# Seams around the up projection: first panels begun inside the output projection, x1 streamed by tile, tails in pieces

## The chip, the cores and the metric

One core of a Trainium2 chip runs one layer of a streaming encoder in one launch. The metric is the device time of one execution in microseconds (us). The median of three timed runs of the kernel before is 2146.97 us, from 2144.51 to 2148.34. Beside these runs one execution was profiled; its trace is what the rows below come from.

## The reference

There are 1152 rows of 1024 values (1024 of a new stream, 8 x 16 of running streams), in float32. The mixers (gated linear attention and differential attention) make `mixed`; what the change touches comes behind them:

```python
x = layer_norm(ALPHA * x + mixed @ w_out, ln1_g, ln1_b)      # w_out 1024 x 1024
up = x @ w_up                                                # w_up 1024 x 5632
a, gate = split(up, [2816])
a_full = concatenate([left, a])                              # left: the last 2 rows of before
a_conv = conv_b
for j in range(3):
    a_conv = a_conv + a_full[:, j:j + t] * conv_w[j]
h = gelu(a_conv) * gate
x = layer_norm(ALPHA * x + h @ w_down, ln2_g, ln2_b)         # w_down 2816 x 1024
ffn_new = a_full[:, -2:]
```

## The kernel before

Every float32 product is made of three matmuls of halves: `split` (lines 91 to 96) makes a rounded high part on ACT (L93, DVE at L95) and the rest on DVE (L96), and `mm3` (lines 86 to 89) issues high x high (L87), one with a low moving part (L88 or L89) and one with a low weight part. So every operand that TensorE reads has first gone through a cast and a subtraction.

The order of the instructions on each engine is fixed when the program is built: a scheduler in the tile framework takes the program as written and sets, engine by engine, what stands behind what. At run time each engine goes through its own list and waits where a semaphore tells it to. A tile pool with n buffers lets the writer of use n+1 wait for the readers of the first. TensorE does matmuls and transposes; ACT casts, copies out of PSUM and does the gelu; DVE subtracts, adds and convolves; POOL does additions and small copies; SP issues all DMAs in one queue.

Output projection (lines 745 to 836). Nine row tiles t of 128 rows. `o_prep(t)` loads `mr`, transposes it (L763) and splits it into `mth` and `mtl`. The eight k slices of w_out come through two `wor` buffers (L797) and are split into `woh` and `wol`. For each tile two PSUM tiles `opp` of 512 columns take 24 matmuls each. DVE adds the residual (L812), `layer_norm` follows (L736, L737), `x1_d` receives the tile (L817), and the tile is transposed (L822). Up to row 576 the transpose is split into the operands of products 1 and 2, and is also copied to `r11` and `r12`; from there on it goes to `r21` and `r22` (L830). POOL forms sums and differences of these (L833 to L836), in place.

Up projection (lines 839 to 914). Rows and inner dimension are halved, and the a and gate columns of one panel take the place of the halves of a matrix product with seven products instead of eight. For each of 22 panels f, `ra` and `rg` bring 128 columns of a and 128 of gate (512 KB each, L852 and L854, two buffers `raw`). POOL forms four weight sums (L858 to L861), which with three unchanged blocks are the weights of products 1, 2, 6, 5, 7, 4 and 3; they are split into `wv` (10 buffers). A product is 24 matmuls of 288 columns, in two PSUM tiles (c = 0 and 1): products 1, 6, 7 and 4 accumulate in `ux`, 5 and 3 in `uy`, product 2 in another `uy`. ACT copies the running sum out where it is wanted (L883 to `ab`, L888 and L893 to `gt`, L897 and L899 to `ab`) and DVE adds the other (L886, L894, L901). The a part lies in `ab` (one buffer, with the two rows to its left, L870 and L871); POOL copies its last rows to `tails` (L903, L904); DVE convolves it (L907, L908, two times L910 and L911); the gelu (L912), the gate (L913) and the store to `h_d` (L914) follow. The operands of products 6, 5, 7, 4 and 3 (`xh`, `xl`) are made in front of the loop by ten casts and ten subtractions over the tiles `r11` to `rs1`.

Down projection (lines 920 to 1012). The 22 slices of h and of w_down come in groups of 2, 4, 4, 4, 4 and 4; each group adds to `yacc`, which for the first group starts as x1, loaded at once (4.6 MB, L964), with L972 adding the first matmuls. After each of the first three groups `tails_out` transposes up to eight slices of `tails` (L953) through one PSUM buffer and writes the new convolution rows.

## Time and profile before

| what | us |
|---|---|
| median of three runs | 2146.97 |
| profiled execution | 2142.43 |
| its span | 2140.4 |
| TensorE busy (matmuls) | 2062.1 (96%) |
| DVE busy | 1107.4 (52%) |
| ACT busy | 787.6 (37%) |
| POOL busy | 454.5 (21%) |

The span is the time from the first to the last instruction that the profiler saw; the execution is 2.0 us longer, and the median of the runs is 4.5 us above the profiled one. Busy shares are averages over stages: the first 1200 us are the input projection and the mixers, the output projection goes from 1201 to 1317, the up projection from 1336 to 1834, the down projection from 1837 to 2131. Where TensorE is busy all the time, nothing that the other engines do is seen in the end; where it waits, the wait list tells for whom. Matmul rows start a step apart and overlap, so their spacing, not their duration, is what one costs.

### The profile page before, as it was taken

The page shows a single profiled execution, that of the slowest core. Times are in us where ns is not written, and L with a number is a line of the kernel's source. Part 1 is how long each engine was busy: PE and PEld are TensorE (multiplying, and loading weights), DVE is VectorE, ACT ScalarE, POOL GpSimd, SP SyncE. Part 2 cuts the span into 40 slices and gives each one's busy share as a digit, 9 for nine tenths or more (in the row PEclk, how much of TensorE's full clock was granted, in tenths as well). Part 3 has the DMA queues.
Part 4 walks back from the last instruction along what each step waited for, and adds up shares of the span by engine and source line. Part 5 has one row for each costly group of instructions (what it writes and reads, how often), then busy time and mean ns, then how long its engine had stood idle before and what let it go on. Part 6 is the DMA issues. An engine that isn't in the chain of part 4 may idle for free.

```text
span 2140.4 us, 34421 instructions
## 1 busy us (share of the span) xinstructions
PE 2062.1 (96%) x14088; PEld 1938.4 (91%) x14088; DVE 1107.4 (52%) x1848; ACT 787.6 (37%) x1750; POOL 454.5 (21%) x531
## 2 busy tenths in 40 slices
PE   7999999999999999999999996999999999699998
PEld 7999999999999999999989885999999999588886
DVE  4344444546536363655544376665555655544447
ACT  3233333244434354434545333333333333301122
POOL 0124233110111102201132206332323222000006
PEclk9999999999999999999999998899999999899999
DMA  5214304422132223322351731222222221712222
GB/s 168 56 23 116 99 25 124 124 53 72 53 106 63 82 49 83 92 72 64 40 123 25 238 128 59 71 72 83 72 74 71 72 83 62 266 56 85 85 84 89
DMA packets 186767, 185.30 MB, mean 87 GB/s; under 512 B 9136, under 2 KB 169228, under 8 KB 186594
## 3 DMA queue, kind: packets, MB, share of 16 engines
q1 hardware_dynamic: 186610, 183.11, 29.8%
q8 instruction: 111, 1.82, 0.4%
q14 instruction: 46, 0.38, 0.1%
HBM read 131.10 MB, written 51.98 MB: 86 GB/s over the span
## 4 chain that ended last, share of the span: by engine, by line
PE 85%; DMA 7%; DVE 5%; ACT 1%; issue 1%; POOL 0%; SPq 0%; DVEq 0%; ACTq 0%; POOLq 0%
PE mm L87 11%; PE mm L89 11%; PE mm L88 11%; PE ux L89 4%; PE ux L87 4%; PE ux L88 4%; PE dn L87 4%; PE dn L88 4%; PE dn L89 4%; PE uy L89 3%; PE uy L87 3%; PE uy L88 3%; PE po L657 3%; PE sc L625 2%; DMA out_prompt_diff_k<-krow 2%; PE sc L626 1%
## 5 line engine op out<-in xcount | busy, mean ns | idle before, releaser
L89 PE MATMUL mm<-whi,xl 128*128 128x256 f32 x1368 | 392.5, 287 | 0.0
L88 PE MATMUL mm<-wlo,xh 128*128 128x256 f32 x1368 | 392.1, 287 | 0.0
L87 PE MATMUL mm<-whi,xh 128*128 128x256 f32 x1368 | 391.3, 287 | 0.0
L89 PEld LDWEIGHTS mm<-whi,xl 128*128 128x128 f32 x1368 | 261.3, 191 | 2.6 <-issue 1.2
L88 PEld LDWEIGHTS mm<-wlo,xh 128*128 128x128 f32 x1368 | 261.3, 191 | 2.3 <-issue 1.0
L87 PEld LDWEIGHTS mm<-whi,xh 128*128 128x128 f32 x1368 | 260.8, 191 | 2.2 <-issue 0.6
L87 PE MATMUL ux<-xh,wv 128*128 128x288 f32 x704 | 208.2, 296 | 11.9 <-ACT wv L93 11.9
L89 PE MATMUL ux<-xh,wv 128*128 128x288 f32 x704 | 208.5, 297 | 3.7 <-DVE wv L96 3.7
L88 PE MATMUL ux<-xl,wv 128*128 128x288 f32 x704 | 208.3, 296 | 0.0
L89 PE MATMUL mm<-xh,wlo 128*128 128x384 f32 x576 | 196.2, 342 | 0.0
L87 PE MATMUL mm<-xh,whi 128*128 128x384 f32 x576 | 195.7, 340 | 0.2 <-DVE sg L699 0.2
L88 PE MATMUL mm<-xl,whi 128*128 128x384 f32 x576 | 195.8, 340 | 0.0
L87 PE MATMUL dn<-wdh,hh 128*128 128x512 f32 x396 | 152.6, 392 | 13.4 <-DVE yacc L972 12.1
L87 PE MATMUL uy<-xh,wv 128*128 128x288 f32 x528 | 156.0, 296 | 0.3 <-ACT wv L93 0.3
L88 PE MATMUL dn<-wdl,hh 128*128 128x512 f32 x396 | 154.9, 391 | 0.6 <-DVE wdl L96 0.6
L88 PE MATMUL uy<-xl,wv 128*128 128x288 f32 x528 | 155.4, 295 | 0.0
L89 PE MATMUL dn<-wdh,hl 128*128 128x512 f32 x396 | 154.2, 391 | 1.1 <-DVE hl L96 1.1
L89 PE MATMUL uy<-xh,wv 128*128 128x288 f32 x528 | 155.1, 295 | 0.0
L87 PEld LDWEIGHTS ux<-xh,wv 128*128 128x128 f32 x704 | 133.1, 189 | 12.4 <-ACT wv L93 12.3
L89 PEld LDWEIGHTS ux<-xh,wv 128*128 128x128 f32 x704 | 133.0, 189 | 4.0 <-DVE wv L96 4.0
L88 PEld LDWEIGHTS ux<-xl,wv 128*128 128x128 f32 x704 | 133.2, 189 | 0.0
L632 ACT ACTIVATE e<-sc,mx 128x256 f32<-128x256 f32 (+7 forms) x128 | 94.2, 741 | 90.8 <-DVE mx L628 76.2
(322 smaller groups left out, 4478.7 us busy)
## 6 DMA issues: line engine op xcount, KB each, us to landing
fraw<-in_w_up SPq DMA_DIRECT2D x44, 512.0 KB, 4.1
raw<-in_w_in SPq DMA_DIRECT2D x38, 512.0 KB, 6.3
raw<-in_w_in SPq DMA_DIRECT2D x52, 256.0 KB, 5.6
h_d<-cv SPq DMA_DIRECT2D x22, 576.0 KB, 2.9
hr<-h_d SPq DMA_DIRECT2D x22, 576.0 KB, 5.0
fraw<-in_w_down SPq DMA_DIRECT2D x22, 512.0 KB, 4.9
og_d<-orow SPq DMA_DIRECT2D x4, 1152.0 KB, 10.0
od_d<-od SPq DMA_DIRECT2D x8, 576.0 KB, 3.5
```

Source lines behind the costliest of these rows:

```text
L87: nc.tensor.matmul(ps, lhsT=lh, rhs=rh, start=start, stop=False, skip_group_check=more)
L88: nc.tensor.matmul(ps, lhsT=lh, rhs=rl, start=False, stop=False, skip_group_check=more)
L89: nc.tensor.matmul(ps, lhsT=ll, rhs=rh, start=False, stop=stop, skip_group_check=more)
L625: nc.tensor.matmul(sc[:, c0:c0 + c], lhsT=Q[m][:, iq], rhs=KH[m][:, c0:c0 + c], start=True, stop=False)
L626: nc.tensor.matmul(sc[:, c0:c0 + c], lhsT=Q[m][:, iq], rhs=KLz[m][:, c0:c0 + c], start=False, stop=True)
L632: act(e[:, :nk], scs[m][:, :nk], AF.Exp, bias=mx[:, m:m + 1], accum_out=Z[:, i, m:m + 1])
L657: nc.tensor.matmul(po[:, 0, :], lhsT=wT[:, kt, :], rhs=v[:, kt, vc0:vc0 + P], start=kt == 0, stop=kt == i)
```

## The change

- `wpool` gets three `raw` buffers instead of two; `wor` loads through `raw` and the pool `ow` goes; `r` has three buffers instead of four.
- The PSUM pools change: `opp` (4) and `otp` (4) are shared by the output and the up projection, and the pool `mmp` of the stages before is closed ahead of them. The transposes of `o_prep` for t > 0 go to `otp` instead of `mm`.
- A class `Panel` holds a panel's work in pieces: loads and split of the first two weights (three buffers `w0` in a pool `ue` that is open during the output projection), the weight sums, the products. Panel 0 is loaded behind t = 6, its sums and the load of panel 1 behind t = 7, panel 0's products 1 and 2 stand in front of the last tile's transposes, panel 1's product 1 behind its sums. `wv` for the other five has 7 buffers.
- The operands of product 6 lie in a pool of their own, `r11` too, and are made first.
- x1 is loaded by row tile into two buffers, and the first group writes `yacc` from it; `hh`, `hl`, `wdh` and `wdl` become parts of one tile `hw`; the tails are written in pieces of four slices inside groups 1 to 3, through two PSUM buffers.

In the diff the methods of `Panel` that only repeat the loop body of before are left out.

```diff
-WV = 10
+WV = 7
...
-    wpool = ctx.enter_context(tc.tile_pool(name="wpool", bufs=2, reuse_waits="tile"))
+    wpool = ctx.enter_context(tc.tile_pool(name="wpool", bufs=3, reuse_waits="tile"))
...
+    class Panel:
+        def __init__(self, f):
+            self.f = f
+            ra = wpool.tile([P, D], F32, tag="raw", name="fraw")
+            nc.sync.dma_start(ra.rearrange("p (k n) -> p k n", k=KD), w_up[:, f * P:(f + 1) * P].rearrange("(k p) n -> p k n", p=P))
+            self.W = {}
+            for i, src in ((1, ra[:, :512]), (2, ra[:, 512:])):
+                self.weight(ue, "w0", 3, i, src)
+            self.ra = ra
+
+        def weight(self, pool, tag, bufs, i, src):
+            self.W[i] = pool.tile([P, 2, 512], F32R, tag=tag, name="wv", bufs=bufs)
+            split(self.W[i][:, 0, :], self.W[i][:, 1, :], src)
+
+        def first(self):
+            self.X = [opp.tile([P, 512], F32, tag="opp", name="ux") for _ in range(2)]
+            for _ in self.prod(1, self.X, True):
+                pass
+
+        def first_out(self):
+            f = self.f
+            self.ab = ab = ue.tile([P, SEQ + 2 + NS * 18], F32, tag="ab", name="ab")
+            self.abs_ = ab[:, SEQ + 2:].rearrange("p (s c) -> p s c", c=18)
+            G.memset(ab[:, 0:2], 0.0)
+            G.tensor_copy(self.abs_[:, :, 0:2], ccT[:, f])
+            for c in range(2):
+                nc.scalar.copy(ab[:, 2 + c * HN:2 + (c + 1) * HN], self.X[c][:, :HN])
+            for c in range(2):
+                V.tensor_tensor(ab[:, 2 + c * HN:2 + (c + 1) * HN], ab[:, 2 + c * HN:2 + (c + 1) * HN], self.Y[c][:, :HN], ALU.add)
...
-            raw = ow.tile([P, D], F32, tag="wor", name="wor")
+            raw = wpool.tile([P, D], F32, tag="raw", name="wor")
...
+            if t == 6:
+                panels[0] = Panel(0)
+            if t == 7:
+                panels[0].sums()
+                panels[1] = Panel(1)
+            if t == NT - 1:
+                panels[0].first()
+                panels[0].second()
+                panels[0].first_out()
             nc.sync.dma_start(x1_d[t * P:(t + 1) * P, :], r)
...
+            if t == NT - 1:
+                panels[1].first()
...
-    for i, r in ((6, "r11"), (5, "rs1"), (7, "r21"), (4, "r22"), (3, "r12")):
+    for pool, which in (("xvb", ((6, "r11"),)), ("xvc", ((5, "rs1"), (7, "r21"), (4, "r22"), (3, "r12")))):
...
     for f in range(NF):
+        if f > 1:
+            panels[f] = Panel(f)
+        p = panels.pop(f)
+        if f > 0:
+            p.sums()
+        p.weights()
+        if f > 1:
+            p.first()
+        if f > 0:
+            p.second()
+            p.first_out()
+        p.rest()
...
-            nc.sync.dma_start(yacc, x1_d.rearrange("(t p) c -> p t c", p=P))
...
+            if gi == 0:
+                x1, xn = xn, x1_load(t + 1) if t + 1 < NT else None
...
-                    V.scalar_tensor_tensor(yacc[:, t, cs], yacc[:, t, cs], ALPHA, ps, ALU.mult, ALU.add)
+                    V.scalar_tensor_tensor(yacc[:, t, cs], x1[:, cs], ALPHA, ps, ALU.mult, ALU.add)
...
-        if gi < 3:
-            tails_out(8 * gi, min(8, NF - 8 * gi))
+            if 0 < gi < 4 and t in (2, 6):
+                tails_out(4 * (2 * (gi - 1) + (t == 6)))
```

How the instructions stand is seen at three places. The first is SP's queue at the start of the output projection (`mix_d` is the last store of the mixers, `mr` the input of a row tile). Before, it reads:

```order
L797 DMA wor<-in_w_out 128x1024 x2
L705 DMA mix_d<-gm 128x256
L752 DMA mr<-mix_d 128x1024
L797 DMA wor<-in_w_out 128x1024 x2
L752 DMA mr<-mix_d 128x1024
L797 DMA wor<-in_w_out 128x1024 x2
```

The loads of two row tiles stand between the w_out loads there. In the changed kernel SP's queue reads at the same place:

```order
L901 DMA wor<-in_w_out 128x1024 x3
L705 DMA mix_d<-gm 128x256
L901 DMA wor<-in_w_out 128x1024 x2
L849 DMA mr<-mix_d 128x1024 x4
L930 DMA x_d<-r 128x1024
```

The loads of w_out go out three and two at a time, and those of the row tiles 1 to 4 now stand behind all of them.

The second is ACT at the seam between the output and the up projection, from the last tile's copies on. Before, with `r_12626` as r22, `rs_12627` as rs1, `r_12625` as r21, `r_12623` as r11 and `r_12624` as r12, it reads:

```order
L830 COPY r_12625<-otp 128x4x128
L830 COPY r_12626<-otp 128x4x128
L93 CAST xh_13572<-r_12626 128x1152 x2
L93 CAST xh_13560<-rs_12627 128x1152 x2
L93 CAST xh_13566<-r_12625 128x1152 x2
L93 CAST xh_13554<-r_12623 128x1152 x2
L93 CAST xh_13578<-r_12624 128x1152 x2
L93 CAST wv<-fraw 128x512 x2
L93 CAST wv<-ta 128x512 x2
```

The first weights stand behind the ten casts there. In the changed kernel ACT's list reads, with `r_12635` as r11, `rs_12634` as rs1, `r_12632` and `r_12633` as r21 and r22 and `r_12631` as r12:

```order
L93 CAST wv<-fraw 128x512 x2
L943 COPY r_12632<-otp 128x4x128
L943 COPY r_12633<-otp 128x4x128
L93 CAST xh_13667<-r_12635 128x1152 x2
L93 CAST xh_13677<-rs_12634 128x1152 x2
L93 CAST xh_13683<-r_12632 128x1152 x2
L93 CAST xh_13689<-r_12633 128x1152 x2
L93 CAST xh_13695<-r_12631 128x1152 x2
L93 CAST wv<-ta 128x512 x2
```

The weights of products 1 and 2 (`wv<-fraw`) have moved ahead of the last tile, and r11, which was fourth, is cast first.

The third is POOL in a panel of the up projection, the same eight rows over and over. Before, it reads:

```order
L870 MEMSET ab 128x2
L871 COPY ab<-ccT 128x8x2
L858 TENSOR_TENSOR ta<-fraw 128x512
L860 TENSOR_TENSOR tb<-fraw 128x512
L859 TENSOR_TENSOR ta<-fraw,ta 128x512
L861 TENSOR_TENSOR tb<-fraw,ta 128x512
L903 COPY tails<-ab 128x2
L904 COPY tails<-ab 128x16
```

The four sums (`ta`, `tb`) stand between the clearing of `ab` and the copies to `tails` there. In the changed kernel POOL's list reads:

```order
L795 MEMSET ab 128x2
L796 COPY ab<-ccT 128x8x2
L762 TENSOR_TENSOR ta<-fraw 128x512
L764 TENSOR_TENSOR tb<-fraw 128x512
L821 COPY tails<-ab 128x2
L822 COPY tails<-ab 128x16
L763 TENSOR_TENSOR ta<-fraw,ta 128x512
L765 TENSOR_TENSOR tb<-fraw,ta 128x512
```

Two of the sums have moved behind the `tails` copies, in front of the next clearing of `ab`.

## Rows read from the trace of the kernel before

**Rows 1.** The waits of TensorE: engine, line, awaited: us in total, times, longest.
```profile
PE dn L87 <- DVE yacc L972: 12.1, 1, 12.1
PE ux L87 <- ACT wv L93: 11.9, 1, 11.9
...
PE ft L953 <- DVE tr L954: 5.8, 2, 4.9
...
PE otp L822 <- DVE r L737: 5.3, 1, 5.3
...
PE dn L87 <- ACT hh L93: 1.3, 1, 1.3
```

**Rows 2.** Busy time by stretch (us, PE, PEld, DVE, ACT, POOL, clock, DMA).
```profile
1190.00:1230.00 40.00, 37.83 (x208) 30.52 (x207) 16.58 (x20) 16.19 (x23) 6.64 (x6) 1.00 0.68 212
1317.00:1344.00 27.00, 5.88 (x22) 4.56 (x21) 22.65 (x18) 15.09 (x20) 15.69 (x10) 0.58 0.05 19
1344.00:1800.00 456.00, 456.00 (x3427) 456.00 (x3426) 264.08 (x409) 165.90 (x349) 144.62 (x164) 0.99 0.24 75
```

**Rows 3.** Timeline of a full panel: start, us, engine, line, operation, [idle before].
```profile
1547.86 0.29 PE L87 MATMUL uy<-xh,wv 128*128 128x288 f32 x1
...
1548.44 0.81 DVE L907 TENSOR_SCALAR cv<-ab,cw,cb 128x1024 f32<-128x1024 f32 x1 [3.17 <-ACT ab L897]
...
1550.03 1.28 DVE L910 SCALAR_TENSOR_TENSOR cv<-ab,cw,cv 128x1024 f32<-128x1024 f32 x1
...
1554.02 0.34 DVE L911 SCALAR_TENSOR_TENSOR cv<-ab,cw,cv 128x128 f32<-128x128 f32 x1
...
1555.25 1.17 ACT L912 ACTIVATE cv<-cv 128x1152 f32<-128x1152 f32 x1
1556.32 0.69 ACT L883 COPY ab<-ux 128x288 f32<-128x288 f32 x2
...
1557.66 0.29 PE L87 MATMUL ux<-xh,wv 128*128 128x288 f32 x1
...
1563.42 1.29 POOL L858 TENSOR_TENSOR ta<-fraw 128x512 f32<-128x512 f32 x1 [8.39 <-DMA fraw<-in_w_up]
...
1566.62 1.14 DVE L96 TENSOR_TENSOR wv<-fraw,wv 128x512 fp32r<-128x512 f32 x1
1570.70 0.81 DVE L907 TENSOR_SCALAR cv<-ab,cw,cb 128x1024 f32<-128x1024 f32 x1 [2.94 <-ACT ab L897]
```

**Rows 4.** Timeline of an early panel, DVE and then POOL.
```profile
1389.30 1.10 DVE L907 TENSOR_SCALAR cv<-ab,cw,cb 128x1024 f32<-128x1024 f32 x1 [3.38 <-ACT ab L897]
1390.33 1.32 DVE L908 TENSOR_SCALAR cv<-ab,cw,cb 128x128 f32<-128x128 f32 x1
...
1392.17 2.31 DVE L910 SCALAR_TENSOR_TENSOR cv<-ab,cw,cv 128x1024 f32<-128x1024 f32 x1
...
1397.19 0.34 DVE L911 SCALAR_TENSOR_TENSOR cv<-ab,cw,cv 128x128 f32<-128x128 f32 x1
...
1389.81 1.75 POOL L859 TENSOR_TENSOR ta<-fraw,ta 128x512 f32<-128x512 f32 x1
1391.64 1.76 POOL L861 TENSOR_TENSOR tb<-fraw,ta 128x512 f32<-128x512 f32 x1
```

**Rows 5.** The chain that ended last, start of the output projection: start, us.
```profile
1202.61 6.39 DMA wor<-in_w_out
...
1226.61 0.92 PE opp L87 x4
```

**Rows 6.** Timeline of the seam: ACT, POOL, TensorE.
```profile
1325.12 2.20 ACT L93 CAST xh<-r 128x1152 fp32r<-128x1152 f32 x2
...
1328.88 2.26 POOL L835 TENSOR_TENSOR r<-rs,r 128x512 f32<-128x512 f32 x1
...
1342.97 0.61 PE L89 MATMUL ux<-xh,wv 128*128 128x288 f32 x1 [3.70 <-DVE wv L96]
```

**Rows 7.** DMA issues of the page: count, KB each, us to landing.
```profile
fraw<-in_w_up SPq DMA_DIRECT2D x44, 512.0 KB, 4.1
```

More of the change, by code (lines that the diff above doesn't have):

```diff
@@ L739 @@
     xr_s = ctx.enter_context(ExitStack())
     xv_s = ctx.enter_context(ExitStack())
+    up_s = ctx.enter_context(ExitStack())
     XH, XL = {}, {}
+    panels = {}
     with ExitStack() as os_:
-        opp = os_.enter_context(tc.tile_pool(name="opp", bufs=4, space=PSUM, reuse_waits="tile"))
-        otp = os_.enter_context(tc.tile_pool(name="otp", bufs=2, space=PSUM, reuse_waits="tile"))
+        otp0_s = os_.enter_context(ExitStack())
+        otp0 = otp0_s.enter_context(tc.tile_pool(name="otp0", bufs=2, space=PSUM, reuse_waits="tile"))
@@ L756, in o_prep @@
                 if t == 0:
+                    tp = otp0.tile([P, 512], F32, tag="otp", name="otp")
+                else:
                     tp = otp.tile([P, 512], F32, tag="otp", name="otp")
-                else:
-                    tp = mmp.tile([P, 512], F32, tag="mm", name="mm")
                 tp = tp.rearrange("p (i c) -> p i c", i=4)
@@ L767, in r_load @@
         def r_load(t):
[L768 removed]
+            r = op.tile([P, D], F32, tag="r", name="r", bufs=3)
             nc.sync.dma_start(r, x_rows(t))
@@ L791 @@
         variant(xv, 2)
-        R = {n: xr.tile([P, KD // 2, HT], F32, tag=n, name=n) for n in ("r11", "r12", "r21", "r22", "rs1")}
+        R = {n: xr.tile([P, KD // 2, HT], F32, tag=n, name=n) for n in ("r12", "r21", "r22", "rs1")}
+        R["r11"] = xr1.tile([P, KD // 2, HT], F32, tag="r11", name="r11")
         woh = oc.tile([P, KD, D], F32R, name="woh")
@@ L836 @@
                 G.tensor_tensor(R["r12"][:, :, c], R["r12"][:, :, c], R["r11"][:, :, c], ALU.subtract)
-    ms.close()
+            if t == NT - 1:
+                panels[1].first()
     us_ = ctx.enter_context(ExitStack())
-    xb = xv_s.enter_context(tc.tile_pool(name="xvb", bufs=1, reuse_waits="tile"))
-    for i, r in ((6, "r11"), (5, "rs1"), (7, "r21"), (4, "r22"), (3, "r12")):
-        variant(xb, i)
-        for k in range(0, KD // 2, 2):
-            split(XH[i][:, k:k + 2, :], XL[i][:, k:k + 2, :], R[r][:, k:k + 2, :])
+    for pool, which in (("xvb", ((6, "r11"),)), ("xvc", ((5, "rs1"), (7, "r21"), (4, "r22"), (3, "r12")))):
+        xb = xv_s.enter_context(tc.tile_pool(name=pool, bufs=1, reuse_waits="tile"))
+        for i, r in which:
+            variant(xb, i)
+            for k in range(0, KD // 2, 2):
+                split(XH[i][:, k:k + 2, :], XL[i][:, k:k + 2, :], R[r][:, k:k + 2, :])
+        xr1_s.close()
@@ L921, with x1_load @@
     dn = ctx.enter_context(tc.tile_pool(name="dnp", bufs=6, space=PSUM, reuse_waits="tile"))
-    ft = ctx.enter_context(tc.tile_pool(name="ftp", bufs=1, space=PSUM, reuse_waits="tile"))
+    ft = ctx.enter_context(tc.tile_pool(name="ftp", bufs=2, space=PSUM, reuse_waits="tile"))
+    def x1_load(t):
+        x1 = fp.tile([P, D], F32, tag="x1", name="x1", bufs=2)
+        nc.sync.dma_start(x1, x1_d[t * P:(t + 1) * P, :])
+        return x1
     def down_load(f):
@@ L945, with tails_out @@
     yacc = fc.tile([P, NT, D], F32, name="yacc")
[L947 to L954 removed]
+    def tails_out(f0):
+        fn = min(4, NF - f0)
+        tr = fc.tile([18, 512], F32, tag="tr", name="tr", bufs=2)
+        tp = ft.tile([P, 4, P], F32, tag="ft", name="ft")
+        for j in range(fn):
+            nc.tensor.transpose(tp[:18, j, :], tails[:, f0 + j, :], ident)
+        V.tensor_copy(tr[:, :fn * P], tp[:18, :fn, :].rearrange("p f c -> p (f c)"))
         cols = slice(f0 * P, (f0 + fn) * P)
```

144 lines of the change are left out of this document (68 added, 76 removed).

## Prediction, made before the changed kernel was run

> **What bounds the kernel now.** I read TensorE's waits first, then the busy times by stretch, then the timeline of the three places that the change touches. The list of waits [rows 1] shows where TensorE stands still, and it names two groups that the change aims at. At the seam between output projection and up projection it waits 5.3 us for the last layer norm and 11.9 for the first weight cast; the stretch from 1317 to 1344 holds only 5.88 us of matmuls at a mean granted clock of 0.58 [rows 2], so part of it ran at the lower of the two levels (1.2 and 2.4 GHz). At the down projection it waits 12.1 us for the first accumulation, which waits for the 4.6 MB load of x1, and 5.8 for the tail transposes. In between, the up projection leaves nothing to win: from 1344 to 1800 TensorE is busy 456.00 of 456.00 us [rows 2]. A change can only lose there.
>
> And the cover in that full stretch is short. Product 6 of a panel accumulates into the PSUM tiles of product 1, so it waits until ACT has copied these into `ab`; the copy waits until the convolution of the panel before is done with the one `ab` buffer. One such turn [rows 3]: product 4 ends and product 3 starts at 1547.86; DVE's convolution runs from 1548.44 to the end of its last step at 1554.36, 5.92 us with two weight splits in it; then come the gelu and, at 1556.32, ACT's two copies; product 6 starts at 1557.66. These 9.80 us are 74 matmuls of 0.1325 us each (9.80 / 74). Of them 0.58 pass before the convolution starts, and 1.55 behind it at best (the gelu's 1.17, the first copy's 0.35, and 0.03 between): the convolution may last 9.80 - 0.58 - 1.55 = 7.67 us before TensorE stops. In this panel POOL makes its four weight sums from 1563.42 on, after the convolution and product 6's start.
>
> An early panel shows what these sums cost when they meet the convolution [rows 4]. Two of the four lie beside it, 1.75 and 1.76 us long instead of 1.29; DVE's 128-column step takes 1.32 us, more than the 1024-column step ahead of it; the `ab`-by-`cv` step takes 2.31 instead of 1.28; the chain lasts from 1389.30 to 1397.53, 8.23 us. Two sums cost it 8.23 - 5.92 = 2.31, some 1.15 each. No stall came of it there, as that panel still had 12 more matmuls (the next panel's product 1) ahead of its product 6.
>
> **A. Start of the output projection: +4.** Before, tiles 0 and 1 share each k of w_out as it arrives; a load into one of the two buffers took 6.39 us at 1202.61 [rows 5], and still 37.83 of the 40 us from 1190 to 1230 are busy [rows 2]. After, tile 1 stands behind all but four of tile 0's 48 matmuls, which are 48 x 0.23 = 10.9 us of work (0.92 / 4, the step of a 512-column matmul [rows 5]). With three buffers the five late loads need about two trips of 6.4 us and a cast and split of some 2 behind each (an estimate from the casts' 1.1 in [rows 6]), 17 us in all; the 24 gate matmuls that now stand behind the first transposes cover 24 x 0.115 = 2.8 (half the columns, half the step). That leaves 17 - 10.9 - 2.8 = 3, and the loads for tiles 1 to 4 stand behind those of w_out on SP: I take +4, bounds 0 (the third buffer pays for it) and +8 (the gate's matmuls cover nothing).
>
> **B. Seam to the up projection: -2.** The 12 matmuls of panel 0 that move inside the output projection cost there what they save later. Behind it 60 of panels 0 and 1 (60 x 0.1325 = 8.0 us) stand ahead of tile 8's transposes, which they may hold up by 8.0 less the 5.3 that these wait for the layer norm anyway, 2.7 us. The chain behind is not shortened: POOL's four differences, ten casts on ACT, ten low parts on DVE. The casts now begin with r11, which is the third difference, ready at 1331.14; before, the first cast was at 1325.12, 1.1 us each [rows 6]. So the weights of product 6 come at 1331.14 + 2.7 + 10 x 1.1 = 1344.8, and the low parts behind them. Before, the last wait ended at 1342.97 with 8 matmuls done; after, 60 are done by then, 52 x 0.1325 = 6.9 us more. Of these 1.8 go for 1344.8, and about 3 for low parts that start 6 us later: -2, bounds -9 (nothing is delayed) and +4 (the eight POOL sums of panels 0 and 1, 8 x 1.29 us, get ahead of the differences).
>
> **C. Panels: +29.** POOL's order is now two sums, the two tail copies, two sums, the clearing of `ab`. The tail copies start when product 4 has been copied out, and the clearing waits for the convolution's end, so the last two sums lie beside the convolution by order alone. The first two wait for their load, which with three raw buffers SP issues once the low part of product 3's weights is done; the like of it ends before at 1567.76 [rows 3], 2.4 us ahead of product 4's end (0.58 before 1570.70), and a panel's load lands 4.1 us after its issue [rows 7]. So they start about 1.7 us after product 4's end, in the convolution too. With two sums felt the chain is 8.23, a stall of 8.23 - 7.67 = 0.56 us a panel; with all four at 1.15 it is 5.92 + 4.6 = 10.5, a stall of 2.9. I take three, between the two that the order ties there and all four: 5.92 + 3.45 = 9.37, a stall of 1.7, rounded to 1.6. The sums of panels 4 to 21 meet a convolution, 18 of them: 18 x 1.6 = +29, bounds 0 (the phase is off) and 18 x 2.9 = +52. Nothing else of a panel is longer: the matmuls, the splits and DVE's order stay, and the smaller `wv` pool (7, and 3 for the first two products) costs nothing while the casts come a product ahead.
>
> The Trainium skill, SBUF — State Buffer, section "Who interferes with whom", says that a DVE instruction with two SBUF inputs contends with a GpSimd instruction that reads SBUF, and that whichever comes second waits for the whole of the other. The stretched steps [rows 4] agree with it in that they read SBUF only. Taken strictly, with DVE second each time, four sums would cost 4 x 1.29, the chain would be 11.1 and the term 18 x 3.4 = +61 in place of +29.
>
> **D. Down projection: -14.** The 12.1 us for x1 go, as tile 0's 512 KB are issued ahead of the loads behind them; the 5.8 of the transposes go, as they come four at a time into two PSUM buffers. What is late next is the first matmul, which waited 1.3 us for ACT's `hh` [rows 1] with 4 transposes as cover, and now waits for casts into one merged tile: about 3 more, and 1 for the low parts. -17.9 + 4 = -14, bounds -18 (no new wait) and -8 (loads of x1 by tile come late once or twice).
>
> **Sum.** 4 - 2 + 29 - 14 = +17 on the profiled execution's 2142.4 us, so 2159.4. The median of the runs shown lies 4.5 above that execution; put on it the forecast is 2147 + 17 = **2164 us**, slower. Its own range is 2145 (C at 18 x 0.56 = +10) to 2183 (C at +52, D at -18).
>
> **Rivals.** *The panels stay full, and it is faster.* If the load comes some us later or DVE wins most meetings, the chain stays under 7.67 us and C is 0: 4 - 2 - 14 = -12, 2135 us. For it: a chain of 5.92 leaves 1.75 us free; against it: two sums are tied to the convolution by order, and two made 8.23. It decides at 7.67 us. Chance 0.20. *Each sum is paid in full*: +61 for +29 gives 2147 + 49 = 2196. Against it: in the early panel two sums cost 1.15 each, less than their 1.29. Chance 0.06. *The seam is not begun early*: the first weights or sums hold up POOL and DVE, the longer chain there; B is +4, A is +8, the rest as forecast: 2147 + 8 + 4 + 29 - 14 = 2174. For it: DVE is busy 22.65 of the seam's 27 us and POOL 15.69 [rows 2]. Chance 0.12. The forecast keeps 0.62.
>
> **How the numbers follow.** 0.2% is 4.3 us, about what a measurement of this kernel can tell from no change. Faster: the first rival but for its upper edge, 0.19. Same: that edge and the low end of the forecast, 0.10. Slower: the rest, 0.71. For 8 in 10 the range takes the forecast's own and the seam case whole and the upper part of the first rival: 2138 to 2183.
>
> **What would show it.** A row in TensorE's waits for ACT's copy of product 1 into `ab`, some 18 times at 0.5 to 2.9 us; convolutions 22.8 to 25 us apart instead of 22.26 (1548.44 to 1570.70); the 128-column step at 1.2 us or more in most panels; the x1 wait gone, and one of about 4 us at the first `dn`; idle time of 4 to 8 us at the start of the output projection. Panels still 22.3 apart would make C and the sign wrong; a gap of under 10 us at the seam would make B wrong.

## The result and the profile after

Over four executions each, the changed kernel takes 2196.89 us (2194.22 to 2197.53) and the kernel before 2146.57 (2144.51 to 2148.34): a ratio of 1.0232, with a 95% interval from 1.0215 to 1.0250. It is slower, as forecast, but by 50 us where 17 were forecast, and outside the range. The profiled execution of the changed kernel took 2196.83 us with a span of 2195.1.

TensorE's busy time hides where the 54.7 us between the two spans went, since a matmul that runs at half clock counts as busy. So the next table is worked out from the traces in another way. For each matmul it takes the time from the start of the one before it, less the step that matmuls of that width keep when nothing is in the way (0.1325 us for 288 columns, 0.227 for 512), and sums these excesses by stage. Waits and low clock are both in it. "Ahead" is all that lies ahead of the first `opp` matmul, "seam" the 45 us behind the last, "down" all from the first matmul of the down projection, which is a tail transpose. How high a column stands depends on the steps taken for the narrower matmuls; by another choice the differences between two kernels come out within some 1.5 us of these.

| lost time of TensorE, us | ahead | output projection | seam | up | down | sum |
|---|---|---|---|---|---|---|
| before | 69.0 | 4.9 | 26.6 | 0.3 | 25.0 | 125.8 |
| after | 79.9 | 12.0 | 24.3 | 49.0 | 15.3 | 180.5 |
| difference | +10.9 | +7.1 | -2.3 | +48.7 | -9.7 | +54.7 |
| forecast | none | +4 (A) | -2 (B) | +29 (C) | -14 (D) | +17 |

The waits of TensorE in the changed kernel, in the columns of [rows 1]:

```profile
PE ux L87 <- ACT ab L798: 32.7, 18, 2.3
PE ux L87 <- ACT wv L93: 22.1, 1, 22.1
PE tp L572 <- DMA kc<-in_cache_diff_k: 7.6, 5, 2.5
...
PE opp L87 <- ACT woh L93: 4.2, 2, 2.8
PE dn L87 <- ACT hw L93: 4.2, 1, 4.2
PE dn L87 <- DVE yacc L1040: 3.7, 2, 2.7
PE mm L87 <- ACT dq L233: 3.3, 1, 3.3
```

The first line is the new one, the row that the prediction named: 18 waits for ACT's copy of product 1 into `ab`. The 12.1 us for x1 and the 5.3 for the last layer norm [rows 1] are gone, but the wait for the first weight cast has grown from 11.9 to 22.1.

Two stretches of the changed kernel, in the columns of [rows 2], are the seam and the panels:

```profile
1330.00:1370.00 40.00, 17.90 (x111) 16.46 (x111) 24.68 (x23) 17.31 (x24) 20.39 (x14) 0.72 0.17 53
1370.00:1860.00 490.00, 455.72 (x3326) 451.20 (x3326) 311.07 (x397) 160.59 (x338) 152.72 (x158) 0.98 0.21 68
```

The panels were full before, 456.00 of 456.00 us; now 34.28 of 490.00 are idle, and DVE's share has gone from 264.08 of 456.00 (58%) to 311.07 of 490.00 (63%) for the same work a panel: its steps have become longer.

One panel shows which ones. This is the timeline of DVE, POOL, ACT and TensorE in the changed kernel, to be held against [rows 3]:

```profile
1488.73 0.81 DVE L825 TENSOR_SCALAR cv<-ab,cw,cb 128x1024 f32<-128x1024 f32 x1 [3.39 <-ACT ab L815]
1489.46 1.32 DVE L826 TENSOR_SCALAR cv<-ab,cw,cb 128x128 f32<-128x128 f32 x1
1490.71 1.80 DVE L96 TENSOR_TENSOR wv<-ta,wv 128x512 fp32r<-128x512 f32 x1
1492.43 1.27 DVE L828 SCALAR_TENSOR_TENSOR cv<-ab,cw,cv 128x1024 f32<-128x1024 f32 x1
...
1493.99 1.17 DVE L829 SCALAR_TENSOR_TENSOR cv<-ab,cw,cv 128x128 f32<-128x128 f32 x1
...
1495.44 2.02 DVE L828 SCALAR_TENSOR_TENSOR cv<-ab,cw,cv 128x1024 f32<-128x1024 f32 x1
...
1497.99 0.34 DVE L829 SCALAR_TENSOR_TENSOR cv<-ab,cw,cv 128x128 f32<-128x128 f32 x1
...
1489.15 1.55 POOL L762 TENSOR_TENSOR ta<-fraw 128x512 f32<-128x512 f32 x1 [14.43 <-DMA fraw<-in_w_up]
1490.66 1.29 POOL L764 TENSOR_TENSOR tb<-fraw 128x512 f32<-128x512 f32 x1
...
1493.72 1.29 POOL L763 TENSOR_TENSOR ta<-fraw,ta 128x512 f32<-128x512 f32 x1
1495.09 1.29 POOL L765 TENSOR_TENSOR tb<-fraw,ta 128x512 f32<-128x512 f32 x1
...
1499.43 0.68 ACT L798 COPY ab<-ux 128x288 f32<-128x288 f32 x2
...
1499.86 0.40 PE L87 MATMUL ux<-xh,wv 128*128 128x288 f32 x1 [1.74 <-ACT ab L798]
```

All four weight sums lie beside the convolution, and for each one step of DVE is long: the first 128-column step (1.32 us instead of 0.34), the split (1.80 instead of 0.68), the second 128-column step (1.17 instead of 0.34) and the last `ab`-by-`cv` step (2.02 instead of 1.28). Each ends within 1.1 us behind a sum's end, so it looks as if DVE's step waits out what is left of the sum. The chain lasts from 1488.73 to 1498.33, 9.60 us instead of 5.92, and the cover is 7.67; the difference of 1.93 is the stall (1.74 in the row, which counts from the modelled end of the matmul before, 1.90 by the starts).

Of 22 convolutions, 18 have all four sums beside them, 9.57 to 9.75 us long. The 18 waits behind them come to 35.6 us by the starts, and a first wait of product 5 to 1.7. The other 11.4 us are mostly the clock. Some panels stand 24.3 us apart and six others 25.7 to 26.2; in these six the clock falls just behind the start of product 6. Windows on two of them, in the columns of [rows 2], and the first matmuls of the first:

```profile
1399.20:1402.40 3.20, 3.04 (x12) 3.04 (x13) 2.55 (x4) 0.93 (x3) 0.00 (x0) 0.50 0.86 285
...
1573.30:1576.50 3.20, 3.20 (x15) 3.20 (x14) 1.38 (x4) 0.40 (x1) 0.00 (x0) 0.50 0.94 321
```

```profile
1399.36 0.61 PE L87 MATMUL ux<-xh,wv 128*128 128x288 f32 x1 [2.29 <-ACT ab L798]
...
1400.25 0.44 PE L87 MATMUL ux<-xh,wv 128*128 128x288 f32 x1
1400.49 0.44 PE L88 MATMUL ux<-xl,wv 128*128 128x288 f32 x1
...
1402.62 0.30 PE L88 MATMUL ux<-xl,wv 128*128 128x288 f32 x1
1402.76 0.30 PE L89 MATMUL ux<-xh,wv 128*128 128x288 f32 x1
```

The granted clock is 0.50 there, the lower level. Steps of 0.24 us instead of 0.1325 for about 3.4 us cost some 1.5 us a time, 9 in all (3.4 / 0.24 = 14 steps, times 0.108, times six); the excesses of these steps in the trace come to 1.5 to 1.6 each.

### The profile page after: what moved, and what is told of

The parts are those of the page before. It is cut to its first block, busy times and chain, and to the rows that moved or that the text cites. A ratio compares the mean times of both kernels' runs of the same rounds, so it can differ in the third digit from the quotient of the medians.

```text
span 2195.1 us, 34411 instructions
## 1 busy us (share of the span) xinstructions
PE 2083.5 (95%) x14088; PEld 1953.6 (89%) x14088; DVE 1165.0 (53%) x1848; ACT 785.0 (36%) x1750; POOL 468.3 (21%) x531
## 4 chain that ended last, share of the span: by engine, by line
PE 50%; DVE 11%; DMA 5%; ACT 3%; issue 2%; POOL 1%; SPq 0%; DVEq 0%; ACTq 0%; POOLq 0%
PE mm L87 5%; PE mm L88 5%; PE mm L89 5%; PE ux L87 4%; PE dn L87 3%; PE dn L89 3%; PE dn L88 3%; PE ux L89 3%; PE ux L88 3%; DVE cv L828 3%; DVE wv L96 2%; PE po L657 2%; PE opp L87 1%; PE opp L89 1%; PE opp L88 1%
## 5 line engine op out<-in xcount | busy, mean ns | idle before, releaser
L87 PE MATMUL ux<-xh,wv 128*128 128x288 f32 x704 | 214.2, 304 | 54.8 <-ACT ab L798 32.7
L89 PE MATMUL ux<-xh,wv 128*128 128x288 f32 x704 | 211.6, 301 | 0.0
L87 PEld LDWEIGHTS ux<-xh,wv 128*128 128x128 f32 x704 | 136.1, 193 | 59.5 <-ACT ab L798 37.0
L87 PE MATMUL dn<-hw 128*128 128x512 f32 x396 | 154.2, 396 | 7.9 <-ACT hw L93 4.2
L88 PE MATMUL dn<-hw 128*128 128x512 f32 x396 | 155.3, 395 | 0.0
L89 PE MATMUL dn<-hw 128*128 128x512 f32 x396 | 153.3, 392 | 0.0
L89 PEld LDWEIGHTS ux<-xh,wv 128*128 128x128 f32 x704 | 136.3, 194 | 0.0
L701 POOL TENSOR_TENSOR gm<-gm,sg 128x512 f32<-128x512 f32 (+1 forms) x40 | 50.0, 1251 | 308.9 <-ACT sg L223 139.3
L87 PEld LDWEIGHTS mm<-xh,whi 128*128 128x128 f32 x576 | 108.6, 189 | 5.8 <-ACT dq L233 3.6
L96 DVE TENSOR_TENSOR wlo<-raw,whi 128x1024 fp32r<-128x1024 f32 x62 | 92.2, 1493 | 36.2 <-ACT whi L93 35.9
```

Source lines behind the costliest of these rows:

```text
L87: nc.tensor.matmul(ps, lhsT=lh, rhs=rh, start=start, stop=False, skip_group_check=more)
L88: nc.tensor.matmul(ps, lhsT=lh, rhs=rl, start=False, stop=False, skip_group_check=more)
L89: nc.tensor.matmul(ps, lhsT=ll, rhs=rh, start=False, stop=stop, skip_group_check=more)
L96: V.tensor_tensor(lo, src, hi.bitcast(F32), ALU.subtract)
L701: G.tensor_tensor(gv, gv, e, ALU.mult)
```

## The experiments

The theory is that the POOL sums beside the convolution make DVE's chain longer than its cover, and that this is most of the loss. The rivals are that a buffer count, a load or the mere number of POOL instructions does it. A second question is where the 10.9 us ahead of the output projection and the 7.1 inside it come from, a third whether a part of the change pays by itself. The table has the results. "Chain" is the usual length of a convolution, from its first step to the end of its last, and "sums" how many POOL sums lie beside one (empty where not taken); "one" marks a single execution; kernels whose label begins with b are built on the kernel before, the others on the changed one.

| kernel | chain | sums | ahead | output | seam | up | down | time, us | before beside it | ratio |
|---|---|---|---|---|---|---|---|---|---|---|
| a_half | 7.58 | 2 | 81.5 | 11.8 | 19.8 | 2.7 | 13.4 | 2145.71, one | 2145.20 | |
| a_nosum | 5.92 | 0 | 76.3 | 12.0 | 19.6 | 1.1 | 12.7 | 2138.78, one | 2145.20 | |
| a_wv6 | 5.92 | 0 | 81.4 | 11.5 | 24.3 | 3.0 | 15.6 | 2148.50 | 2145.20 | 1.0020 [1.0006, 1.0034] |
| a_raw2 | 8.81 | 4 | 69.9 | 20.0 | 20.7 | 31.0 | 13.0 | 2171.06 | 2145.20 | 1.0121 [1.0094, 1.0148] |
| a_raw2_wv6 | 5.31 | 0 | 72.1 | 18.2 | 20.3 | 3.9 | 13.5 | 2143.47 | 2143.84 | 1.0001 [0.9990, 1.0013] |
| a_raw2_own_wor | | | 71.2 | 15.6 | 20.1 | 3.5 | 11.6 | 2140.75 | 2143.84 | 0.9987 [0.9976, 0.9998] |
| b_raw3 | | | 77.0 | 4.5 | 27.8 | 0.3 | 25.7 | 2154.03 | 2143.84 | 1.0048 [1.0031, 1.0065] |
| b_down | | | 72.6 | 4.8 | 25.4 | 0.7 | 12.7 | 2132.14 | 2143.84 | 0.9942 [0.9925, 0.9958] |
| a_w02 | 5.92 | 0 | 79.5 | 12.1 | 18.9 | 1.9 | 13.0 | 2142.43 | 2145.27 | 0.9991 [0.9981, 1.0001] |
| a_best_try | | | 67.8 | 18.5 | 20.6 | 1.1 | 13.3 | 2137.93 | 2143.80 | 0.9972 [0.9964, 0.9981] |
| b_psum | | | 73.5 | 15.4 | 27.4 | 0.3 | 24.5 | 2156.40 | 2143.25 | 1.0056 [1.0034, 1.0078] |

Some results lie outside what was expected of them. a_half, a_nosum and a_w02 are 2 to 7 us faster than the lower ends of their ranges, and their seams lose 4.5 to 5.4 us less than the changed kernel's, which no expectation had (the part on B below shows why). a_raw2 is 4 us and b_down 2 us faster than theirs. a_raw2_own_wor and a_best_try came out in the ranges of their rivals, and the chain of a_w02_read is shorter than expected, 7.98 us.

### Fewer sums: a_half and a_nosum

The first makes two of the four sums, and products 7 and 4 use the weights of 5 and 6; the second makes none, and all four use a slice as it was loaded.

```diff
-            G.tensor_tensor(tb[:, 0, :], b22, b12, ALU.subtract)
-            G.tensor_tensor(tb[:, 1, :], b21, ta[:, 1, :], ALU.subtract)
-            self.T = ((6, ta[:, 1, :]), (5, ta[:, 0, :]), (7, tb[:, 0, :]), (4, tb[:, 1, :]), (3, b22))
+            self.T = ((6, ta[:, 1, :]), (5, ta[:, 0, :]), (7, ta[:, 0, :]), (4, ta[:, 1, :]), (3, b22))
```

> The changed kernel without two of POOL's four weight sums per panel (tb is not made; products 7 and 4 take the weights of 5 and 6, so their values are not the kernel's). Theory (sums beside the convolution): the chain on DVE falls from 9.6 us to about 8, near the 7.67 us that TensorE covers, so the 18 waits for ACT's copy into ab fall from 32.7 us in all to under 9 and the short low-clock stretches go with them: 2197 - 35 to 49 = 2148 to 2162 us. Rival (the chain is late because the two weight splits in it wait for ACT's casts, with the smaller wv pool): splits and casts stay as many, so the chain stays at 9 us or more and the time above 2185.

> The changed kernel without any of the four weight sums (products 6, 5, 7 and 4 take the block b12 as their weights, so their values are not the kernel's). Theory: with nothing of POOL beside it the chain on DVE is 5.9 to 6.6 us, as in a full panel of before, no wait for the copy into ab is left, panels are 22.3 us apart: 2146 to 2150. What is left over 2146.6 is then not the panels' doing: about +11 before the output projection and +7 in it, less about 2 at the seam and 10 at the down projection. Rival (casts): chain still 9 us.

With two sums the chain is 7.58 us, just inside the cover, and 46 of the 49 us lost in the up projection are gone; of the 18 waits for `ab`, 32.7 us in all, two are left, 0.5 us in all. The chains that are a little longer show where the cover ends: behind chains of 7.64, 7.68, 7.86 and 7.90 us the next began 22.33, 22.37, 22.56 and 22.60 us later instead of 22.27. Each of these distances is longer than 22.27 by what its chain has over 7.58 us. (One distance of 22.62 behind a chain of 7.58 is not of this kind: a_memset, with chains of 5.92, has it at the same panel.) So the cover is 7.58 us, and the 7.67 that the prediction worked out from one panel holds to a tenth of a microsecond. Two weight splits lie in the chain of a_nosum as in that of the changed kernel, so the rival that these splits wait too long for their casts is out. With no sums the chain is the 5.92 of before. A sum beside the convolution costs (7.58 - 5.92) / 2 = 0.83 us or (9.60 - 5.92) / 4 = 0.92. Steps of one chain of a_half, DVE and then POOL:

```profile
1496.08 1.32 DVE L823 TENSOR_SCALAR cv<-ab,cw,cb 128x128 f32<-128x128 f32 x1
...
1497.93 1.27 DVE L825 SCALAR_TENSOR_TENSOR cv<-ab,cw,cv 128x1024 f32<-128x1024 f32 x1
...
1499.49 1.02 DVE L826 SCALAR_TENSOR_TENSOR cv<-ab,cw,cv 128x128 f32<-128x128 f32 x1
...
1495.91 1.40 POOL L761 TENSOR_TENSOR ta<-fraw 128x512 f32<-128x512 f32 x1 [13.99 <-DMA fraw<-in_w_up]
...
1498.02 2.34 POOL L762 TENSOR_TENSOR ta<-fraw,ta 128x512 f32<-128x512 f32 x1
```

Here the second sum met the `ab`-by-`cv` step that had begun before it (1497.93), kept its 1.27, and it was the sum that became longer: 2.34. The next 128-column step (1499.49) then met the rest of that sum and took 1.02 us instead of 0.34.

### The sums elsewhere, with nothing left out: a_wv6 and a_w02

One buffer fewer, of the later weights in the first and of the first two weights in the second. All sums are made.

```diff
-WV = 7
+WV = 6
```

```diff
-                self.weight(ue, "w0", 3, i, src)
+                self.weight(ue, "w0", 2, i, src)
```

> The changed kernel with 6 instead of 7 buffers for the weights of the last five products; nothing is left out. On POOL the order then is tails, three sums, clearing of ab, the fourth sum, and no longer two sums, tails, two sums, clearing. Theory: what counts is where the sums meet the convolution. Here three still stand between the tails and the clearing, but they come with a weight split less in need, so the wait falls, to between 0 and 1 us a panel: 2148 to 2175. Rival (a smaller wv pool makes the casts late, and that is the stall): one buffer less makes it worse, over 2200.

> The changed kernel with two in place of three buffers for the first two products' weights, 7 wv buffers as in the change; nothing is left out. On POOL all four sums then stand behind the clearing of ab and ahead of the next tails. Theory (their place decides): convolutions of 5.9 to 6.6 us, panels 22.3 apart, no wait for the copy into ab; the 10 us of the three raw buffers stay: 2144 to 2152. Rival (the stall comes with the number of wv buffers, 7 against 6): panels stay at 24.3, 2190 to 2200.

Either edit takes away 46 to 47 us of the loss in the up projection. In both the scheduler puts the load of the panel's gate half elsewhere in SP's queue, and the sums follow it. In the changed kernel that load is issued at 1485.37, 3.4 us ahead of the convolution's start at 1488.73. In a_wv6 it is issued behind the start at 1500.19, and in a_w02 behind 1493.08 (SP and POOL, of a_wv6 and then of a_w02):

```profile
1501.89 0.37 SPq L758 DMA_DIRECT2D fraw<-in_w_up  x1
...
1506.06 1.81 POOL L762 TENSOR_TENSOR ta<-fraw 128x512 f32<-128x512 f32 x1 [5.00 <-DMA fraw<-in_w_up]
```

```profile
1499.68 0.37 SPq L758 DMA_DIRECT2D fraw<-in_w_up  x1
...
1503.42 1.58 POOL L762 TENSOR_TENSOR ta<-fraw 128x512 f32<-128x512 f32 x1 [3.76 <-DMA fraw<-in_w_up]
```

The sums now begin at the end of the chain or behind it (it ends at 1506.10 and 1499.00). So where they lie decides, not their number. That a_w02 keeps all seven `wv` buffers shows that their count is not the cause by itself: each edit moved the load by way of the schedule.

### Two raw buffers again: a_raw2 and a_raw2_wv6

```diff
-    wpool = ctx.enter_context(tc.tile_pool(name="wpool", bufs=3, reuse_waits="tile"))
+    wpool = ctx.enter_context(tc.tile_pool(name="wpool", bufs=2, reuse_waits="tile"))
```

> The changed kernel with two raw buffers in place of three; nothing is left out. Theory for the 11 us that the changed kernel loses ahead of the output projection: the third raw buffer lets the scheduler order the loads and transposes of the first 1200 us otherwise; with two, the first opp matmul is back at 1201 to 1203 instead of 1212. The start of the output projection gets worse, +5 to +9 over the changed kernel's, as w_out now passes through two buffers that mr needs as well. The panel stall remains in part (two sums still stand behind the tails): 0.5 to 2 us a panel. In sum 2175 to 2200. Rival (the early loss comes of the PSUM pools): the first opp matmul stays near 1212.

> The changed kernel with two raw buffers and 6 wv buffers. Theory: the 10 us of the first stages come back (two raw), the panels run at 22.25 to 22.4 us (the sums fall otherwise), the output projection keeps the 8 us that two raw buffers cost beyond the changed kernel's: 2148.5 - 10 + 8 = 2140 to 2150. Rival (with two raw buffers the sums meet the convolution whatever the number of wv buffers, as they did with 7): panels of 23 to 23.8, 2160 to 2175.

Three things move at once in a_raw2. The stages ahead of the output projection get back 10.0 us (79.9 to 69.9), the output projection loses 8.0 more, and the panels lose 31.0 instead of 49.0. Four sums lie beside each chain still, but none of the splits, and what stalls most is another product:

```profile
PE uz L87 <- DVE gt L819: 17.3, 14, 1.3
...
PE ux L87 <- ACT ab L798: 4.8, 6, 2.9
```

With six `wv` buffers beside it the sums leave the convolution here too (chain 5.31, 3.9 us lost in the panels), and the kernel is level with the one before.

### What the third raw buffer costs by itself: b_raw3

```diff
-WV = 10
+WV = 9
...
-    wpool = ctx.enter_context(tc.tile_pool(name="wpool", bufs=2, reuse_waits="tile"))
+    wpool = ctx.enter_context(tc.tile_pool(name="wpool", bufs=3, reuse_waits="tile"))
```

> The kernel before with three raw buffers (and 9 instead of 10 wv buffers, to make room); nothing else. Theory (the third raw buffer alone makes the first 1200 us longer): first opp matmul at 1209 to 1214 instead of 1201, panels still 22.25 apart, 2146 + 8 to 12 = 2154 to 2159. Rival (the early loss belongs to the other parts of the change): first opp matmul at 1201 to 1203, 2145 to 2149.

It is 10.2 us slower than the kernel before, and 8.0 of it lies ahead of the output projection (77.0 against 69.0). Over all profiles the two cases do not overlap there: 67.8 to 73.5 us lost in the seven tabled kernels with two raw buffers, before included, and 76.3 to 81.5 in the six with three, the changed kernel included. `wpool` serves all stages, and its buffer count orders those of the first 1200 us anew. The loss there is made of small waits, such as the 7.6 us for `kc` and the 3.3 for `dq` in the changed kernel's list, and of the clock. In the changed kernel TensorE's waits in the first 1200 us come to 30.5 us instead of 24.9, and there are two stretches of 3.4 us at half clock, at 627.7 and 815.5, with TensorE busy throughout; by half their length they cost about 3 us. The kernel before has none there. Which reordering causes which wait was not followed further.

### The output projection: a_raw2_own_wor, a_best_try and b_psum

The first two give `wor` a pool of its own again beside two raw buffers and six `wv`; the second has three `r` buffers instead of two, and two `w0`.

```diff
+        ow = os_.enter_context(tc.tile_pool(name="ow", bufs=2, reuse_waits="tile"))
...
-            raw = wpool.tile([P, D], F32, tag="raw", name="wor")
+            raw = ow.tile([P, D], F32, tag="wor", name="wor")
```

The third is the kernel before with only the PSUM pools of the output projection as the change has them.

```diff
+        otp0 = otp0_s.enter_context(tc.tile_pool(name="otp0", bufs=2, space=PSUM, reuse_waits="tile"))
...
-                    tp = mmp.tile([P, 512], F32, tag="mm", name="mm")
+                    tp = otp.tile([P, 512], F32, tag="otp", name="otp")
...
+        ms.close()
+        opp = os_.enter_context(tc.tile_pool(name="opp", bufs=4, space=PSUM, reuse_waits="tile"))
+        otp = os_.enter_context(tc.tile_pool(name="otp", bufs=4, space=PSUM, reuse_waits="tile"))
```

> The changed kernel with two raw buffers, w_out in a pool of its own again (two wor buffers), 6 wv buffers and two r buffers. Theory on the start of the output projection: its loss comes of w_out going through the raw buffers, so TensorE's lost time from the first to the last opp matmul falls from the 20.0 of two raw buffers to 5 to 9. Rival (it comes of the order: tile 1 can no longer share the k slices as they arrive, since its transposes need the PSUM that the gates hold): 13 to 20 are left. The first 1200 us are as before, the panels free of stalls; 2131 to 2137 by the theory, 2138 to 2146 by the rival.

> The changed kernel with two raw buffers, w_out in its own two wor buffers, three r buffers as in the change, two buffers for the first two weights and 6 wv buffers: what the runs so far point to, taken together. Theory: the first stages as before (first opp matmul at 1201 to 1205), no stall in the panels (three sums and the fourth stand where DVE's convolution is over), seam and down projection keep their gains; the wait of 7.5 us for a tile of r in the run with two r buffers goes, which leaves 7 to 9 us of lost TensorE time in the output projection: 2126 to 2133, at or a little under the version with the down projection alone. Rival (the loss there is in the order of tiles 0 and 1, whatever the buffers): 12 or more are left there, 2134 to 2140.

> The kernel before with only the PSUM pools of the output projection as in the change: the pool mm closed ahead of it, opp (4) and otp (4) opened behind the last gate, the transposes of tiles 1 to 8 into otp. Buffers raw, wor and r stay as before. Theory (the loss at the start of the output projection is the order: tile 1 no longer shares the k slices of w_out, since its transposes have no PSUM until the gates are through): TensorE's lost time from the first to the last opp matmul rises from 4.9 to 11 to 16, and the time by as much: 2150 to 2156. Rival (it is the buffers: w_out through raw): lost time stays at 5 to 7, 2143 to 2147.

The own pool does not bring the output projection back: 15.6 and 18.5 us are lost. In both a wait of 7.4 us stands where TensorE's list has tile 0's transposes ahead of tile 1's matmuls, with three `r` buffers as with two, so the `r` buffers are not its cause. The PSUM pools alone put the same wait into the kernel before (the wait list, and TensorE's timeline behind tile 0):

```profile
PE otp L826 <- DVE r L737: 13.7, 2, 7.4
```

```profile
1240.12 1.97 PE L826 MATMUL otp<-ident,r 128*128 128x128 f32 x8 [7.42 <-DVE r L737]
```

They raise the loss in the output projection from 4.9 to 15.4. In the changed kernel itself this wait does not appear: there the 28 us from 1212 on hold 23.56 us of matmuls, TensorE waits 4.2 us for w_out's casts, and the clock is low for 3.4 us at 1221.7. So the pools by themselves cost 10.5 us in the kernel before; that the 7.1 of the changed kernel come from them too was not shown.

### The part that pays: b_down

The kernel before with the changed down projection alone: x1 by tile, `hw`, the tails in pieces and two `ft` buffers.

```diff
-            nc.sync.dma_start(yacc, x1_d.rearrange("(t p) c -> p t c", p=P))
+            xn = x1_load(0)
...
-        if gi < 3:
-            tails_out(8 * gi, min(8, NF - 8 * gi))
+            if 0 < gi < 4 and t in (2, 6):
+                tails_out(4 * (2 * (gi - 1) + (t == 6)))
```

> The kernel before with the down projection of the changed kernel (x1 by row tile, one merged hw tile, tails in pieces) and nothing else. Theory: this part alone is worth what the changed kernel gains there, 25.0 - 15.3 = 9.7 us of TensorE's lost time; the wait of 12.1 for x1 goes, a wait of 4 to 5 for the first hw cast comes: 2145.5 - 8 to 11 = 2134 to 2138. Rival (the seam into the down projection only looks better because the changed up projection stalls and leaves loads time): gain under 4 us.

> The kernel before with the changed down projection alone once more, beside the run above on the same chip: 2129 to 2135, ratio to before 0.993 to 0.996.

It is the fastest kernel of this study, 2132.14 us and in a second set 2133.18 (ratio 0.9946, from 0.9930 to 0.9963). The down projection loses 12.7 us instead of 25.0, a gain of 12.3. In the changed kernel the same edit gains 9.7: there the first `dn` waits 4.2 us for `hw`, and in b_down 1.6 (TensorE's waits of b_down):

```profile
PE ft L955 <- DVE tr L956: 3.9, 1, 3.9
...
PE dn L88 <- DVE hw L96: 1.6, 1, 1.6
```

In the changed kernel ACT casts the first slice of h into `hw` at 1904.19, behind the last gelu at 1902.19, which waits for the last convolution; in b_down TensorE is at work on `dn` at 1840.36, ahead of that gelu at 1841.80.

### Busy or reading: a_memset, a_w02_read and a_w02_write

These ask what of a POOL instruction DVE feels. a_memset writes constants in place of the four sums. The other two leave the sums as they are in a_w02 and add work beside the convolution: three products that read and write SBUF, or eight writes of a constant.

```diff
-            G.tensor_tensor(ta[:, 0, :], b12, b11, ALU.subtract)
+            G.memset(ta[:, 0, :], 0.5)
```

```diff
+            jk = uc.tile([P, 512], F32, tag="jk", name="jk")
+            G.memset(jk, 0.0)
+            G.tensor_copy(jk[:, 0:2], ab[:, SEQ:SEQ + 2])
+            for _ in range(3):
+                G.tensor_tensor(jk, jk, jk, ALU.mult)
```

> The changed kernel with each of POOL's four weight sums replaced by a constant written into the same tile (the weights of products 6, 5, 7 and 4 are constants, so their values are not the kernel's). POOL still writes four 512-column tiles per panel, two of them between the tails and the clearing of ab by order, but reads nothing. Theory (a step of DVE with its operands in SBUF and a POOL instruction that reads SBUF take turns): the convolution is 5.92 to 6.3 us although POOL works beside it. Rival (any work of POOL beside DVE lengthens it, reads or not): about 0.9 us for each write beside it, 7 us or more.

> The kernel with two buffers for the first two weights (no stall in its panels, convolutions of 5.92 us), with three added 512-column products on POOL per panel that read and write a tile of their own; they stand behind the tails and ahead of the clearing of ab, so beside the convolution. Nothing is left out. Theory (SBUF reads of POOL and DVE take turns): each costs the convolution about 0.92 us as the weight sums do, 8.4 to 8.9 us, a stall of 0.7 to 1.3 in 20 panels: 2155 to 2172. Rival (the sums delay the convolution through what they make, not by being there): 5.92 us, 2141 to 2147.

> The same with eight added constant writes on POOL per panel into that tile in place of the three products: about the same POOL time beside the convolution (8 x 0.53 us), but nothing is read. Theory: the convolution stays at 5.92 to 6.2 us, 2141 to 2147. Rival (any work of POOL beside DVE lengthens it): 8 us or more, 2155 to 2172.

Each of the three was run once. a_memset (2144.10 us, chain 5.92) tells nothing on this question: the schedule put its writes almost wholly behind the convolution. The other two answer it. One chain of a_w02_read (first fence) and one of a_w02_write (second), DVE and then POOL:

```profile
1499.30 1.52 DVE L96 TENSOR_TENSOR wv<-ta,wv 128x512 fp32r<-128x512 f32 x1
1500.74 2.06 DVE L833 SCALAR_TENSOR_TENSOR cv<-ab,cw,cv 128x1024 f32<-128x1024 f32 x1
...
1503.09 0.76 DVE L834 SCALAR_TENSOR_TENSOR cv<-ab,cw,cv 128x128 f32<-128x128 f32 x1
...
1499.13 4.57 POOL L827 TENSOR_TENSOR jk<-jk 128x512 f32<-128x512 f32 x3
```

```profile
1496.25 1.27 DVE L833 SCALAR_TENSOR_TENSOR cv<-ab,cw,cv 128x1024 f32<-128x1024 f32 x1
...
1497.81 0.34 DVE L834 SCALAR_TENSOR_TENSOR cv<-ab,cw,cv 128x128 f32<-128x128 f32 x1
...
1495.46 4.62 POOL L827 MEMSET jk<- 128x512 f32 x8
```

Three products make the chain 7.98 us, 2.06 more than a_w02's, 0.69 each; 4.62 us of POOL writes in the same place leave it at 5.93, and the time at 2143.16 beside 2143.25. So POOL being busy costs DVE nothing; reading does. The chain of 7.98 lies over the cover, and its kernel takes 2157.57 us, with 14.3 lost in the up projection and panels 22.67 us apart, 0.40 more than 22.27, as 7.98 is more than 7.58.

The Trainium skill, SBUF — State Buffer, section "Who interferes with whom", has it so: a DVE instruction with two SBUF inputs contends with a GpSimd instruction that reads SBUF and not with one that only writes it. 5.93 against 7.98 agrees. The trace has more than this sentence: the first 128-column step has one tensor as its input and is stretched by a sum too (1.32 us instead of 0.34).

## Why the forecast was right in sign and wrong in size

**C, the panels: the mechanism was right, the term too small, +48.7 for +29.** The wait, its place, the number of panels (18) and, to a tenth of a microsecond, the cover came out as said. The order on POOL was read rightly too: the load was issued 2.8 us ahead of product 4's end (2.4 forecast), and the first sum began 1.0 behind it (1.7 forecast). Three sums felt at 1.15 each were forecast; four were felt, at 0.92, which makes nearly the same chain (9.60 for 9.37) and a stall of 1.98 us for 1.6, so 35.6 us. The 1.15 was read too high: in that early panel the end of a third sum lay beside the chain's first step, which took 1.10 us instead of 0.81 [rows 4]. Without these 0.29 us the two sums cost 1.01 each. The third sum, in the kernel before:

```profile
1388.56 1.29 POOL L860 TENSOR_TENSOR tb<-fraw 128x512 f32<-128x512 f32 x1
```

The step that failed is the product 18 x 1.6 as the whole of the term. It left out that a wait of this length can bring the clock down behind it; six half-clock stretches and smaller losses make up the other 13.

The strict reading, that each sum costs its full 1.29 us, forecast a total of 2196, and the total came out there. But it says a chain of 11.1 and a stall of 3.4, and neither was seen: the agreement of the totals is an accident. DVE waits for what is left of a running sum, and where it came first, the sum waited. The rival that the panels stay full is what a_half, a_wv6 and a_w02 show: the cover decides, at 7.58 us where 7.67 was forecast.

**Ahead of the output projection: no term, +10.9.** This is the step that was missing. The prediction costed the third raw buffer at the start of the output projection, where it should help, and never asked what else draws on that pool. b_raw3 loses 8.0 more there with that buffer (and one `wv` fewer), and a_raw2 gets 10.0 back without it.

**A, the start of the output projection: +7.1 for +4,** inside its bounds of 0 and +8, and by the way that was forecast, waits for the loads of w_out and their casts. The clock's 3.4 us at 1221.7 were not in it.

**B, the seam: -2.3 for -2, in part by luck.** One wait of 22.1 us for the casts has taken the place of three, 11.9 and 5.3 [rows 1] and 3.70 [rows 6], 20.9 in all. More was to be had: in seven of the experiments on the changed kernel the seam loses 18.9 to 20.7. What the changed kernel has beyond them is a wait on ACT that the forecast did not have. In it the last tile's transposes end at 1345.5, but two weight casts stand ahead of ACT's copies of them, and these wait for their load (first fence, ACT). In a_w02 the copies go first (second fence):

```profile
1350.28 1.14 ACT L93 CAST wv<-fraw 128x512 fp32r<-128x512 f32 x2 [10.59 <-DMA fraw<-in_w_up]
1351.33 1.06 ACT L943 COPY r<-otp 128x512 f32<-128x512 f32 x2
1356.44 2.21 ACT L93 CAST xh<-r 128x1152 fp32r<-128x1152 f32 x2 [4.05 <-POOL r L948]
```

```profile
1345.14 1.07 ACT L943 COPY r<-otp 128x512 f32<-128x512 f32 x2 [3.11 <-PE otp L935]
```

Counted from the last `opp` matmul, the ten casts begin at 20.1 us in the changed kernel and at 14.5 in a_w02, where the forecast had 17.0; product 6 begins at 31.3 and at 25.7, where it had about 31. So the chain itself was forecast some 5 us too long, and a wait that was not forecast took the 5 us back.

**D, the down projection: -9.7 for -14.** The waits of 12.1 and 5.8 us went as said, and the first `dn` waits 4.2 us instead of 1.3, 2.9 more where 4 were forecast. But TensorE now waits twice for DVE's sums into `yacc`, 3.7 us, and ahead of the first tail transposes, 1.1: -17.9 + 2.9 + 3.7 + 1.1 = -10.2, near the -9.7. The forecast took no wait for `yacc` as its value, only as a bound. b_down, where the wait for `hw` is 1.6, has -12.3.

The missing 10.9 and the 20 missing in C explain the 38 us between 17 and the 54.7 of the spans, with 3 from A, 4 from D and nothing from B. Each of the four terms lies inside its own bounds. The time lies above the range because the fifth term was missing and because the range's upper end, 2183, puts the highest C beside the lowest D: with D at its -8 it is 2193.

**Not settled.** Which reordering of the first 1200 us costs the 8 to 10 us was not followed; nor what distinguishes the six panels whose clock fell from the twelve whose clock did not.

## What to carry to other kernels

Where an engine has no idle time, work out the cover of the chain that feeds it to a tenth of a microsecond (7.58 here, 7.67 by the sum) and ask of every helper instruction whether its place lies inside that chain: the same four sums cost 49 us there and next to nothing some 10 us later. A buffer count is an order in disguise: one `wv` buffer fewer gained 48 us by the order that it brought, not by what it buffers. One shared raw buffer more cost 10, presumably in the same way, which was not shown. So split a change of several parts and run the parts by themselves; here one of them gains 0.55% and the whole loses 2.3%.

## What the runs showed of the hardware

- A short wait in an otherwise full stretch can cost nearly twice its length. After six of 18 waits of 1.9 to 2.5 us the granted clock was 0.50 for about 3.4 us, which cost 1.5 to 1.6 us each time; behind the other twelve it stayed at 1.00. In the panels of a_raw2 fourteen waits of 1.4 us drew no such stretch, and only the first wait, of 3.1 us, did.
- DVE's steps and POOL's sums wait for each other, and the later one pays: a 128-column step took 1.32 us instead of 0.34, and a sum 2.34 instead of 1.29. DVE's chain became 0.69 to 0.92 us longer for each POOL instruction of 128x512 float32 that reads (a_w02_read, a_half, the changed kernel), and 0.01 us for all eight that only write (a_w02_write).
